# Layer B's Strassen blocks in a written order, with sums by adding DMA

## The chip, the cores and the metric

The kernel runs on one core of a Trainium2 chip. The metric is the device time of one execution in microseconds (us). TensorE (PE) multiplies, VectorE (DVE), ScalarE (ACT) and GpSimd (POOL) work elementwise, SyncE (SP) issues DMAs; ACT and GpSimd issue some, too. Everything is in float32.

## The reference

Two layers, each h = h + W_out(mixer(RMSNorm(h)) * silu(z)), and a last RMSNorm. The sequence has 1024 tokens, the model 1024 channels, the inner width is 2048. Layer A gates chunks of 128 tokens; layer B is a Mamba-2 mixer. What matters here is the input projection of layer B and what stands right behind it:

```python
proj = h @ w_in                                   # 1024 x 1024 times 1024 x 6176
z = proj[..., :D_INNER]                           # gate: silu(z)
xbc = proj[..., D_INNER:D_INNER + B_CONV_DIM]     # x, B and C
dt_raw = proj[..., D_INNER + B_CONV_DIM:]
xbc = jax.nn.silu(causal_depthwise_conv(xbc, conv_w, conv_b))   # 4 taps along the tokens
dt = jax.nn.softplus(dt_raw + dt_bias)            # then cumulative sums and decays per chunk of 128
```

Then a scan over eight chunks in eight groups uses x, B, C, dt and silu(z), a group norm follows, and the output projection.

## The kernel before, in words

A float32 product is made of three matmuls: each operand is split into a high part (a cast, `split`, L106, ACT) and a low part (source minus high part, VectorE; L112), and `mm3` (L131) adds high x high, high x low and low x high in PSUM.

The projections of layer A and most of layer B's are done in **blocks** of Strassen-Winograd (class `Block`, L182). A block multiplies four quarters of the weights, b[kh, j] (each 512 rows by 256 columns, one tile of 128 x 4 x 256 from a ring of four `wr` slots, L193), with quarters and sums of quarters of the transposed, normalized activations (A11 to A22, S1 to S4; high and low part, fourteen tiles out of the sixteen slots of tag s8). Instead of eight products there are seven, numbered 1 to 7, each of two **units** of twelve matmuls (128 x 128 x 512). Seven products need weight sums: t1 = b01 - b00 (L204, product 5), t2 = b11 - t1 (L205, product 6), b10 - t2 in place (L212, product 4), b11 - b01 in place (L214, product 7). `prep` (L207) makes the sums that a product needs, casts and subtracts; `mm` (L222) runs a unit; `post` (L247) copies a PSUM partial result to SBUF (`u`, L252, products 1, 6 and 7) or hands a finished quarter to `done` (products 2, 4, 5 and 3). Products 1, 6, 7 and 4 add up in the same two PSUM banks, 5 and 3 in two others, 2 in two of its own. `run` (L264) loads the four quarters and takes the products in the order 1, 2, 6, 7, 4, 5, 3.

Layer B has eight such blocks:

- gate blocks 0 to 3 (`z_block`, L905; `zb`), whose `done` adds the two partial results (VectorE, L913), applies silu (ACT, L915) and stores to `z_d` by a DMA that GpSimd issues (L917). Gate block 3 has half the columns (one unit per product);
- x, B and C blocks for two pairs of groups (`xbc_block`, L1214; an x block and a B/C block for each pair). Their `done` adds (VectorE, L1240), copies a halo of three columns (ACT, L1244) and puts a convolution on the list `todo`: one ACT instruction (L1211), three taps on VectorE (L1205, each with a small halo instruction L1208 for the second half of the tokens), silu on ACT (L1234) and a store that ACT issues (L1235). Two of the eight convolutions of a block read their input straight from PSUM. `convolve` (L1196) does one from the list.

`into_b` (L959), the end of layer A, gate block 0, and products 1 of gate block 1, is one `manual_schedule`: each engine takes its instructions in the order in which they are written. What follows (L1191, L1192 and L1335 to L1347) is left to the compiler's scheduler, which picks an order for each engine: the rest of gate block 1 with `decays` (L1142, small vectors from dt) behind product 6, gate block 2, then x pair 0, B/C pair 0, x pair 1, gate block 3, B/C pair 1, with a convolution before each unit from x pair 0 on. Gate block 1 and 2 make their sums on VectorE, the later ones on GpSimd, where gate block 3 also makes its low parts. `rest_a21` (L1257) reloads and splits A21. Up to LEFT = 4 convolutions are left for the scans. Then comes a new PSUM pool (L1348), the projections that are not done by Strassen (`projections`, L1274, tile `ab`) and the scans (L1570), written out by hand again.

In layer A's and B's output projection (class `Out`, L618) there are already sums by DMA: `add` (L701, L702) issues from GpSimd a DMA with `accum_op`, which adds its source to the destination, and L699 and L667 negate a tile on ACT for it.

Names: P = 128; tag k2 has three slots (tiles zt, xc), q4 six (u), wh and wl three each. `tk` holds per-token vectors for the scans in an s8 slot to the end.

## Time and profile before

| | us |
|---|---|
| median of 3 runs (1626.3 to 1628.99) | 1627.37 |
| the profiled execution | 1622.94 |
| its span, first to last instruction | 1621.2 |
| TensorE busy | 1514.6 |
| VectorE, ACT, GpSimd busy | 1085.5, 757.0, 466.8 |

Times in rows count from the start of the span. A row of a group gives line, engine, operation, output<-inputs, shapes and count, then busy us and mean ns of one, then the idle time of the engine just before them and what ended it. A row of a timeline gives start, length, engine and instruction; in brackets the idle time before it. A row of waits gives who waited for whom: us in total, times, longest. A row with three figures between strokes gives the shortest, median and longest duration in ns.

### The profile page before, as it was taken

The page shows a single profiled execution, that of the slowest core. Times are in us where ns is not written, and L with a number is a line of the kernel's source. Part 1 is how long each engine was busy: PE and PEld are TensorE (multiplying, and loading weights), DVE is VectorE, ACT ScalarE, POOL GpSimd, SP SyncE. Part 2 cuts the span into 40 slices and gives each one's busy share as a digit, 9 for nine tenths or more (in the row PEclk, how much of TensorE's full clock was granted, in tenths as well). Part 3 has the DMA queues.
Part 4 walks back from the last instruction along what each step waited for, and adds up shares of the span by engine and source line. Part 5 has one row for each costly group of instructions (what it writes and reads, how often), then busy time and mean ns, then how long its engine had stood idle before and what let it go on. Part 6 is the DMA issues. An engine that isn't in the chain of part 4 may idle for free. (4 is left out here: it accounts for less than half of the span.)

```text
span 1621.2 us, 21245 instructions
## 1 busy us (share of the span) xinstructions
PE 1514.6 (93%) x7832; PEld 1246.8 (77%) x7832; DVE 1085.5 (67%) x1669; ACT 757.0 (47%) x1239; POOL 466.8 (29%) x477
## 2 busy tenths in 40 slices
PE   5899999999999999997899998999999999889988
PEld 4799988888888878775678776777777767657776
DVE  6966566666666545577743788587777777657646
ACT  4522232333223345554543454456666576544454
POOL 3601110000000131234203223316766766221231
PEclk9899999999999999998999999999999999979999
DMA  5153333233334999932253222547666665795993
GB/s 171 44 185 135 106 98 109 101 104 109 109 109 167 297 263 238 191 104 65 83 108 113 83 98 85 175 134 206 172 173 183 171 188 143 228 239 179 223 241 113
DMA packets 164872, 244.89 MB, mean 151 GB/s; under 512 B 16048, under 2 KB 96800, under 8 KB 161568
## 3 DMA queue, kind: packets, MB, share of 16 engines
q1 hardware_dynamic: 134672, 166.43, 34.1%
q0 software_dynamic: 20928, 63.45, 17.2%
q10 hardware_dynamic: 9168, 13.64, 2.3%
q8 instruction: 62, 1.02, 0.3%
q14 instruction: 42, 0.34, 0.1%
HBM read 169.23 MB, written 51.18 MB: 136 GB/s over the span
## 5 line engine op out<-in xcount | busy, mean ns | idle before, releaser
L134 PE MATMUL acc<-hh,wh 128*128 128x512 f32 x868 | 345.3, 398 | 14.5 <-ACT wh L111 4.2
L135 PE MATMUL acc<-hl,wh 128*128 128x512 f32 x868 | 342.8, 395 | 4.4 <-DVE hl L989 4.4
L136 PE MATMUL acc<-hh,wl 128*128 128x512 f32 x868 | 342.5, 395 | 3.8 <-DVE wl L112 3.0
L112 DVE TENSOR_TENSOR wl<-wr,wh 128x1024 fp32r<-128x1024 f32 x94 | 122.9, 1310 | 128.8 <-ACT wh L111 128.8
L134 PEld LDWEIGHTS acc<-hh,wh 128*128 128x128 f32 x868 | 165.8, 191 | 52.0 <-DVE u L1240 5.2
L136 PEld LDWEIGHTS acc<-hh,wl 128*128 128x128 f32 x868 | 165.8, 191 | 41.3 <-DVE wl L112 4.8
L135 PEld LDWEIGHTS acc<-hl,wh 128*128 128x128 f32 x868 | 165.9, 191 | 38.7 <-DVE hl L989 4.8
L111 ACT CAST wh<-wr 128x1024 fp32r<-128x1024 f32 (+1 forms) x113 | 116.2, 1030 | 115.8 <-PE acc L135 78.7
L252 ACT COPY u<-acc 128x512 f32<-128x512 f32 x117 | 68.0, 582 | 187.2 <-PE acc L136 185.9
L136 PE MATMUL acc<-wh,hl 128*128 128x256 f32 x448 | 131.3, 293 | 11.5 <-DVE hl L355 11.5
L134 PE MATMUL acc<-wh,hh 128*128 128x256 f32 x448 | 132.1, 295 | 4.2 <-DVE vt L291 2.5
L135 PE MATMUL acc<-wl,hh 128*128 128x256 f32 x448 | 130.7, 292 | 1.1 <-DVE wl L365 1.1
L1424 ACT ACTIVATE wl<-wl,tk 128x128 f32<-128x128 f32 x256 | 82.1, 391 | 88.2 <-DMA wl<-cs_d 87.7
L134 PE MATMUL ab<-hh,wh 128*128 128x512 f32 x256 | 115.5, 451 | 2.2 <-DVE u L1240 2.2
L136 PE MATMUL ab<-hh,wl 128*128 128x512 f32 x256 | 100.8, 394 | 0.0
L135 PE MATMUL ab<-hl,wh 128*128 128x512 f32 x256 | 100.1, 391 | 0.0
L136 PEld LDWEIGHTS acc<-wh,hl 128*128 128x128 f32 x448 | 89.9, 201 | 12.5 <-DVE hl L355 12.5
L134 PE MATMUL bo<-wh,xh 128*128 128x512 f32 x192 | 80.9, 421 | 14.6 <-ACT wh L111 5.7
L134 PEld LDWEIGHTS acc<-wh,hh 128*128 128x128 f32 x448 | 90.0, 201 | 5.2 <-issue 2.9
L112 DVE TENSOR_TENSOR xl<-ya,xh 128x1024 fp32r<-128x1024 f32 x40 | 49.1, 1228 | 64.3 <-ACT xh L111 64.2
L135 PEld LDWEIGHTS acc<-wl,hh 128*128 128x128 f32 x448 | 90.0, 201 | 1.6 <-DVE wl L365 1.4
L605 POOL DMA_DIRECT2D y_d<-y x8 | 4.4, 548 | 291.8 <-DVE y L602 291.8
(316 smaller groups left out, 3379.6 us busy)
## 6 DMA issues: line engine op xcount, KB each, us to landing
wr<-in_a_w_in_dram SPq DMA_DIRECT2D x48, 512.0 KB, 3.6
wl<-cs_d SPq DMA_DIRECT2D x64, 256.0 KB, 3.6
wr<-in_b_w_in_dram SPq DMA_DIRECT2D x30, 512.0 KB, 4.8
ya<-ya POOLq DMA_DIRECT2D x28, 512.0 KB, 14.7
wb<-in_a_w_out_dram SPq DMA_DIRECT2D x10, 1024.0 KB
wb<-in_b_w_out_dram SPq DMA_DIRECT2D x10, 1024.0 KB, 18.2
wr<-in_b_w_in_dram SPq DMA_DIRECT2D x36, 256.0 KB, 4.4
v<-v_d SPq DMA_DIRECT2D x8, 1024.0 KB, 4.9
```

Source lines behind the costliest of these rows:

```text
L111: nc.scalar.copy(out=hi, in_=src)
L112: return (eng or nc.vector).tensor_tensor(out=lo, in0=src, in1=hi.bitcast(F32), op=ALU.subtract)
L134: nc.tensor.matmul(out=o, lhsT=l[0], rhs=r[0], start=start, stop=False, **kw)
L135: nc.tensor.matmul(out=o, lhsT=l[0], rhs=r[1], start=False, stop=False, **kw)
L136: nc.tensor.matmul(out=o, lhsT=l[1], rhs=r[0], start=False, stop=stop, **kw)
L252: nc.scalar.copy(out=self.u[n][:, i], in_=a)
L605: store = lambda: nc.gpsimd.dma_start(out=y_d[-1], in_=y)
L1424: nc.scalar.activation(wl[:, j, :], wl[:, j, :], AF.Relu, scale=-1.0, bias=tokc(2, c, self.g)[:, j:j + 1])
```

## The change

The blocks of layer B behind gate block 0 are written out by hand with into_b in one `manual_schedule`. The order of blocks becomes gate 1, x pair 0, gate 2, B/C pair 0, gate 3, x pair 1, B/C pair 1; that of the products 1, 2, 6, 7, 5, 4, 3. Each product's cast and low part are written one product ahead. The sums are made by DMA, begun in the block before: `sums_a` (at product 7) negates b01 into t2 and in place on ACT and adds b00 to t2 and b11 to b01; `sums_b` (at product 5) negates b00 into t1 and adds b01 to it, and b11 to t2; `fourth` (at the block's own product 2) writes -t2 over b10 and adds b10 again from HBM. The weights of the next block are loaded between its products. t1 and t2 share one s8 tile, t12, in all blocks; those of gate block 1 are issued at the end of into_b. Gate stores of blocks 1 to 3 are issued by ACT instead of GpSimd. A convolution is begun in every second unit, and its silu and store follow in the next unit (`late`). `decays` and `rest_a21` become generators whose pieces stand between units; the tiles of `decays` move from s8 to q4. LEFT becomes 3.

```diff
 class Block:
+        def add(self, dst, kh, j):
+            o = 0
+            for w in self.W(kh, j):
+                n = w.shape[1]
+                nc.gpsimd.dma_start(out=dst[:, :, o:o + n], in_=w.rearrange("(k p) n -> p k n", p=P),
+                                    accum_op=ALU.add)
+                o += n
+        def sums_a(self):
+            b12 = self.b[0, 1]
+            t12 = s8([P, 2, 4, 256], "t12")
+            self.t1, self.t2 = (t12[:, i, :, :self.cols] for i in range(2))
+            nc.scalar.mul(self.t2, b12, -1.0)
+            nc.scalar.mul(b12, b12, -1.0)
+            self.add(self.t2, 0, 0)
+            self.add(b12, 1, 1)
+        def sums_b(self):
+            nc.scalar.mul(self.t1, self.b[0, 0], -1.0)
+            self.add(self.t1, 0, 1)
+            self.add(self.t2, 1, 1)
+        def fourth(self):
+            b21 = self.b[1, 0]
+            nc.scalar.mul(b21, self.t2, -1.0)
+            self.add(b21, 1, 0)
...
         def prep(self, n, lo=None):
+            if self.eng is not None:
+                self.sum_up(n)
...
-            nc.gpsimd.dma_start(out=z_d[g][:, m, th * 512:(th + 1) * 512], in_=zt)
+            (nc.scalar if b else nc.gpsimd).dma_start(out=z_d[g][:, m, th * 512:(th + 1) * 512], in_=zt)
...
-    SPILT, AHEAD, LEFT = (0, 1, 3, 5), 16, 4
+    SPILT, AHEAD, LEFT = (0, 1, 3, 5), 16, 3
...
         dt_post(0, pd)
+        nxt.sums_a()
+        nxt.sums_b()
         for i in range(2):
             blk.post(3, i), nxt.post(1, i)
...
-        dtw = s8([P, 6, 256], "dtw")
+        dtw = q4([P, 4, 256], "dtw")
+        cs = q4([P, 256], "cs")
...
-    zb[1].run((2, 6, 7, 4, 5, 3), {6: decays})
-    zb[2].run()
...
     def convolve():
+        while late:
+            late.pop(0)()
         if todo:
-            todo.pop(0)()
+            late.append(todo.pop(0)())
...
-            nc.scalar.activation(dst, dst, AF.Silu)
-            nc.scalar.dma_start(out=xbc_d[g][:, th, m, :], in_=dst)
+            def rest():
+                nc.scalar.activation(dst, dst, AF.Silu)
+                nc.scalar.dma_start(out=xbc_d[g][:, th, m, :], in_=dst)
+            return rest
...
-        xbc_block("x", gs).run(unit=convolve)
-        if gs[0]:
-            zb[3].eng = nc.gpsimd
-            zb[3].run(unit=convolve, lo=nc.gpsimd)
-        xbc_block("bc", gs).run(behind={6: rest_a21, 5: lambda: next(pj)} if gs[0] else {},
-                                unit=convolve)
+    def blocks():
+        ORDER = (1, 2, 6, 7, 5, 4, 3)
...
+        bs = [zb[1], xbc_block("x", pairs[0]), zb[2], xbc_block("bc", pairs[0]), zb[3], xbc_block("x", pairs[1]),
+              xbc_block("bc", pairs[1])]
+        seq = [(k, n) for k in range(len(bs)) for n in ORDER]
+        small, turn, a21 = decays(), [0], rest_a21()
+        def between():
+            turn[0] += 1
+            if next(small, 0) == 0 and turn[0] % 2:
+                convolve()
+            else:
+                while late:
+                    late.pop(0)()
+        for at, (k, n) in enumerate(seq[1:], 1):
+            b, nxt = bs[k], bs[k + 1] if k + 1 < len(bs) else None
+            if at + 1 < len(seq):
+                k2_, n2 = seq[at + 1]
+                if n2 not in bs[k2_].Y:
+                    bs[k2_].prep(n2)
+            if n == 2:
+                b.fourth()
+            if nxt is not None:
+                if n == 1 or at == 1:
+                    nxt.load(0, 1)
+                if n == 6:
+                    nxt.load(0, 0)
+                elif n == 7:
+                    nxt.sums_a()
+                elif n == 5:
+                    nxt.load(1, 0)
+                    nxt.sums_b()
+                elif n == 4:
+                    nxt.load(1, 1)
+            elif n == 7:
+                next(a21)
+            elif n == 4:
+                next(a21, None)
+                next(pj)
+            for i in range(b.units):
+                between()
+                b.mm(n, i)
+        while len(todo) > LEFT:
+            convolve()
+    with tc.manual_schedule():
+        into_b()
+        blocks()
     next(pj)
-    while len(todo) > LEFT:
-        convolve()
```

More of the change, by code (lines that the diff above doesn't have):

```diff
@@ L207, in prep, with sum_up @@
         def prep(self, n, lo=None):
+            b = self.b
+            if self.eng is not None:
+                self.sum_up(n)
+            src = {1: b[0, 0], 2: b[1, 0], 4: b[1, 0], 7: b[0, 1], 3: b[1, 1]}.get(n)
+            if src is None:
+                src = self.t1 if n == 5 else self.t2
+            h_, l_ = wh([P, 4, self.cols]), wl([P, 4, self.cols])
+            split(h_, l_, src, lo)
+            self.Y[n] = (h_, l_)
+        def sum_up(self, n):
             b, TT = self.b, self.eng.tensor_tensor
@@ L1134 @@
     zb[0].eng, zb[0].wide = nc.gpsimd, True
-    with tc.manual_schedule():
-        into_b()
     tok_of = {}
@@ L1147, in decays @@
         nc.scalar.activation(e_, e_, AF.Exp)
+        yield
         V.tensor_scalar(s_, e_, 2.0, None, ALU.add)
@@ L1153, in decays @@
         for k in range(7, 0, -1):
+            if k == 4:
+                yield
             V.scalar_tensor_tensor(p_, p_, 1.0 / (2 * k + 1), s2, ALU.add, ALU.mult)
+        yield
         V.scalar_tensor_tensor(p_, p_, 1.0, s_, ALU.add, ALU.mult)
@@ L1187, in decays @@
             nc.scalar.copy(out=tok[:, i], in_=tp[:, 0:256].rearrange("p (c r) -> p c r", c=2))
+            yield
         nc.sync.dma_start(out=decb, in_=dec_d.rearrange("c h -> (c h)").partition_broadcast(P))
         tok_of.update(tok=tok, decb=decb)
-    zb[1].run((2, 6, 7, 4, 5, 3), {6: decays})
-    zb[2].run()
-    xbc_d, todo = {}, []
+    xbc_d, todo, late = {}, [], []
     def convolve():
+        while late:
+            late.pop(0)()
         if todo:
-            todo.pop(0)()
+            late.append(todo.pop(0)())
     def conv_ops(dst, src, ch, halo=None):
@@ L1259, in rest_a21 @@
         nc.sync.dma_start(out=raw, in_=f01_d)
+        yield
         H2.update(new_H(("A21",)))
@@ L1590, in scans @@
         project(AHEAD // 2 + 1)
-        while todo:
+        while todo or late:
             convolve()
```

22 lines of the change are left out of this document (8 added, 14 removed).

## The prediction

> **What bounds the kernel now.** I read the page first, then the windows over the stage that the diff touches, then TensorE's waits there, then the order of time around one wait.
>
> ```profile
> span 1621.2 us, 21245 instructions
> PE 1514.6 (93%) x7832; PEld 1246.8 (77%) x7832; DVE 1085.5 (67%) x1669; ACT 757.0 (47%) x1239; POOL 466.8 (29%) x477
> ```
> TensorE is busy 93% of the span, so a gain has to come out of its holes. The stage runs from the second product of gate block 1 to the first matmul of the projections:
>
> ```profile
> 799.80:1066.90 267.10, 250.93 (x1075) 203.15 (x1073) 178.84 (x234) 125.66 (x191) 68.76 (x49) 0.98 0.39 113
> ```
> ```profile
> 799.14 0.39 PE L134 MATMUL acc<-hh,wh 128*128 128x512 f32 x1
> ...
> 799.82 0.39 PE L134 MATMUL acc<-hh,wh 128*128 128x512 f32 x1
> ...
> 830.55 0.39 PE L136 MATMUL acc<-hh,wl 128*128 128x512 f32 x1
> 834.54 0.80 PE L134 MATMUL acc<-hh,wh 128*128 128x512 f32 x1 [3.60 <-DVE zt L913]
> 835.13 0.63 PE L135 MATMUL acc<-hl,wh 128*128 128x512 f32 x1
> ...
> 837.56 0.40 PE L135 MATMUL acc<-hl,wh 128*128 128x512 f32 x1
> ```
> The columns of the window are us, then busy time of PE, PEld, DVE, ACT, POOL, then clock, DMA share and GB/s. The code issues 89 units of 12 matmuls here (12 of gate block 1, five full blocks of 14, 7 of the half-size gate block 3): 1068. The two rows at 799 are three matmuls apart, 0.68/3 = 0.227 us each at full clock, so the stage needs 242.4 us. It takes 267.1: **24.7 us are lost**, and no more can be won here. The rows from 830.55 on show what a loss is made of: 7.01 us to 837.56 where eight matmuls need 1.81, that is 5.2 lost, of which 3.60 idle and 1.6 in matmuls that run at about half the clock behind the hole (0.63 in place of 0.39).
>
> ```profile
> PE acc L134 <- DVE u L1240: 4.0, 3, 2.9
> PE acc L134 <- DVE zt L913: 3.6, 1, 3.6
> PE acc L134 <- ACT wh L111: 2.8, 1, 2.8
> PE acc L134 <- ACT u L252: 2.7, 2, 1.6
> PE ab L134 <- DVE u L1240: 2.2, 1, 2.2
> ```
> These waits sum to 15.3; slow matmuls behind three of them, six transposes (1.2) and short hitches make up the rest. Their releasers are post-processing and casts, not VectorE's or GpSimd's sums as such.
>
> **The change part by part.** Durations that the steps use (busy, mean ns, idle before):
>
> ```profile
> L111 ACT CAST wh<-wr 128x1024 fp32r<-128x1024 f32 x31 | 32.3, 1049 | 29.5 <-PE acc L135 21.6 <-POOL t L204 2.4 <-PE acc L136 2.2
> L252 ACT COPY u<-acc 128x512 f32<-128x512 f32 x38 | 22.0, 579 | 16.3 <-PE acc L136 15.1 <-ACT xc L1234 1.2
> L1211 ACT ACTIVATE xc<-u,par 128x512 f32<-128x512 f32 x22 | 17.8, 811 | 2.9 <-DMA xbc_d<-xc 2.4 <-ACT xc L1234 0.4
> L1234 ACT ACTIVATE xc<-xc 128x512 f32<-128x512 f32 x28 | 17.7, 631 | 41.7 <-DVE xc L1208 34.3 <-DVE xc L1205 7.4
> L913 DVE TENSOR_TENSOR zt<-acc,u 128x512 f32<-128x512 f32 x15 | 10.2, 686 | 17.8 <-DMA z_d<-zt 10.5 <-PE acc L136 7.3
> L112 DVE TENSOR_TENSOR wl<-wr,wh x10: 1212/1221/1227, 780.2 to 850.6; 128x1024 fp32r<-128x1024 f32 x10
> L699 ACT ACTIVATE wb<-wb x8: 1061/1062/1065, 596.3 to 1505.7; 128x1024 f32<-128x1024 f32 x8
> ```
> *Sums.* Four tensor_tensor per block leave GpSimd and VectorE. In their place come four negating copies on ACT (1.06 each, the L699 row) and five adding DMAs. VectorE's other work gains by that, too:
>
> ```profile
> 907.53 2.83 POOL L214 TENSOR_TENSOR wr<-wr 128x1024 f32<-128x1024 f32 x1
> ```
> ```profile
> 908.04 2.33 DVE L1208 SCALAR_TENSOR_TENSOR xc<-halo,par,xc 128x2 f32<-128x2 f32 x1
> 910.30 0.74 DVE L1205 SCALAR_TENSOR_TENSOR xc<-u,par,xc 128x509 f32<-128x509 f32 x1
> 910.96 0.21 DVE L1208 SCALAR_TENSOR_TENSOR xc<-halo,par,xc 128x3 f32<-128x3 f32 x1
> 911.09 0.73 DVE L1205 SCALAR_TENSOR_TENSOR xc<-acc,par,xc 128x511 f32<-128x511 f32 x1
> ```
> The two-column end of a tap took 2.33, until GpSimd's sum was through; the next one 0.21. So I count a tap with its halo at 911.09-910.30 = 0.79 and without at 910.96-910.30 = 0.66: three make 2.4 and 2.0. Without the GpSimd sums VectorE has no other reason to be slow, and no price of its own in the sum.
>
> *Entry.* The new sums of block 1 start only at the end of into_b, behind dt_post on ACT:
>
> ```profile
> 793.78 1.03 ACT L953 ACTIVATE dtr<-part,hv 32x256 f32<-32x256 f32 x2 [1.28 <-DVE part L950]
> ```
> ```profile
> L702 POOL DMA_DIRECT2D wb<-wb x16: 831/1190/3217, 574.9 to 1520.5; - x16
> ```
> ```profile
> wb<-wb POOLq DMA_DIRECT2D x2, 512.0 KB, 6.7
> ```
> ```profile
> DMA to landing us min/median/max: 4.6/14.0/24.2
> ```
> The first negation ends at 794.8+1.1 = 795.9. t2 then needs two adds in a row, the second waiting on GpSimd for the first. No add runs in this stage yet: over the whole kernel the landings range from 4.6 to a median of 14.0. The DMA is busy 0.39 of this stage, so I take the 6.7 of the window from 1440 to 1480, nearer to the short end. t2 is whole at 809.3; the cast (1.05) and low part (1.22) of product 6 end at 811.6, while product 2 ends on TensorE at 799.8+24x0.227 = 805.2. That is 6.4 idle and 1.6 of slow clock, **8 us** that before does not have (2.2 with landings of 4.6, 23 with 14). [...] Queued behind the waiting cast on ACT stand the posts of product 2; nothing else waits for those.
>
> *Later sums* are begun a block ahead: from the step of product 5, where t1 and t2's last add are issued, to the cast of product 6 lie four products, 21.8 us, against two landings of 6.7 to 14; the fourth sum has three products, 16.3, against one negation and one landing. Hidden in full-size blocks; if landings were 14, some 1 us per block would show.
>
> *The written order.* Before, a scheduler filled ACT and VectorE; now each takes its instructions as written. What that does is seen in into_b, already written:
>
> ```profile
> 783.20 0.63 ACT L915 ACTIVATE zt<-zt 128x512 f32<-128x512 f32 x1 [7.40 <-issue]
> 786.21 0.63 ACT L915 ACTIVATE zt<-zt 128x512 f32<-128x512 f32 x1 [2.38 <-DVE zt L913]
> 786.75 1.04 ACT L111 CAST wh<-wr 128x1024 fp32r<-128x1024 f32 x1
> ```
> The first row is a silu that waits for its product; the cast of the next block at 786.75 stands behind it and behind a second silu, and starts when that is through. And a store issued by ACT costs it about 0.4:
>
> ```profile
> 933.72 0.33 ACTq L1235 DMA_DIRECT2D xbc_d<-xc  x1
> 934.09 0.59 ACT L252 COPY u<-acc 128x512 f32<-128x512 f32 x1 [0.40 <-ACT xc L1234]
> ```
> The gate stores move there from GpSimd. A product lasts 24x0.227 = 5.45. In gate block 2 six of the seven products also carry a convolution of the block before, begun in the first unit. ACT's pass from one cast to the next is then, for products 2 and 5: cast 1.05, negation 1.06, convolution's first 0.81, taps 2.4 and VectorE's add 0.69 (the silu behind them waits), three silus with stores 3x1.03 = **9.1**. Product 7: cast 1.05, low part 1.22 (t12 has one free slot beside fourteen activation tiles and tk, so the negation waits for the last reader), two negations 2.1, 0.81, 2.4, silu and store 1.03, copy 0.58 = 9.2. Product 4: 1.05+1.22+2.4+2x1.03 = 6.7. Products 1 and 6: 1.05+1.22+2.0+1.03+0.58 = 5.9. Product 3: 5.45. Sum 51.3 against 38.1: 13.2 late, less the 2.3 by which a low part is early at the start: 10.9. The single waits that this makes, product by product, are at most some 3.5 us, of the size of the idle above; I count one slow clock for them, 1.6, and take **12 us** (6 if the waits overlap half as much, 18 with a slow clock behind four). Gate block 3 has products of 2.72, with four convolutions and the full-size negations of the next block: casts 7x0.6 (an estimate: half of 1.05 and some start-up), negations 0.6+3x1.06, copies 3x0.58, outputs 4x1.03, convolutions 4x1.84 = 21.2 of ACT in 19.1 of TensorE, 2 us over even without a wait; with the same waits on taps and on t12, which come four times in half the time, I take **8 us** (4 to 14).
>
> [...]
>
> ```profile
> 912.48 0.80 PE L134 MATMUL acc<-hh,wh 128*128 128x512 f32 x1 [2.89 <-DVE u L1240]
> 913.08 0.63 PE L135 MATMUL acc<-hl,wh 128*128 128x512 f32 x1
> ```
> *The rest.* In the four x/B/C blocks ACT has no silus of its own: 2 us in all (0 to 6). The transposes stay at 1.2. The hand-over stays near its 2.2 to 2.6 (to 10 if three convolutions written ahead of the projections hold PSUM). The small vectors of the decays fit into the units; as many table loads as before come with them.
>
> *Sum.* 8+12+8+2+1.2+2.6 = 33.8 lost instead of 24.7: **9 us slower**. Outside the stage I take nothing: one convolution fewer is left over. The profiled execution took 1622.94 (span 1621.2), so 1632; the median of the three runs lies 4.4 above it, so 1636 in their terms.
>
> **The rivals.** (a) *ACT's queue keeps up.* It decides at passes of 5.45+2.3/7 = 5.8 on average in the gate blocks. For it: ACT was busy only 125.66 of 267.10, and one adds roughly 28 of negations and 10 of stores, 61%. Against it: the passes above are latency, not load. Then 12 and 8 shrink to 2 each, 18 lost, 7 faster; with landings of 4.6 at the entry and none in the gate blocks 2.2+2+1.2+2.6 = 8 lost, 16 faster: 1611 to 1620. (b) *The sums land late*: landings of 14 give entry 23 and 1 us in each of six blocks, 21 more: 1657. Against it: 0.39 of DMA share. (c) *Even*: the losses trade, 24.7 again, 1627. (d) *The sums are not begun a block ahead*, because a slot of the weights comes free a product later than written: three products, 16.3, then stand against two landings, 13.4, still hidden, so 1636; it is in the forecast's chance.
>
> **How the numbers follow.** Forecast 0.48; (a) 0.32; (b) 0.08; (c) 0.12. A measurement tells about 0.2% (3.3 us) from no change, so (c) is "same": faster 0.32, same 0.12, slower 0.56. The range leaves out (b) and the far end of (a): 1613 to 1650. The forecast alone: 1631 to 1650.
>
> **What would show it.** Right: TensorE waits at about 805 for a cast of t2; waits on ACT casts and low parts in gate blocks 2 and 3, none to speak of in x/B/C; ACT idle behind the taps. Wrong: gate block 2 at 39 us; GpSimd's adds landing past 10 us; slow clock in x/B/C blocks; or time moved in the scans.

## The result and the profile after

| us | before | after |
|---|---|---|
| median of 4 runs each on one chip | 1626.84 (1623.89 to 1628.99) | 1673.03 (1668.48 to 1675.64) |
| ratio | 1 | 1.0282 (95%: 1.0253 to 1.0312) |
| span of the profiled execution | 1621.2 | 1673.8 |
| from the last dt matmul (L978, before L943) to the first projection matmul | 278.2 | 327.2 |
| behind it | 554.3 | 558.4 |

The change is slower by 46 us, against 9 forecast: outside the range of 1613 to 1650. The two profiled executions lie further apart than the medians: of 52.6 us more span, 49.0 lie in the stage and 4.1 behind it (-0.5 ahead). The page of the changed kernel begins:

```profile
span 1673.8 us, 21300 instructions
PE 1521.9 (91%) x7832; PEld 1249.4 (75%) x7832; DVE 1052.5 (63%) x1668; ACT 784.3 (47%) x1267; POOL 456.4 (27%) x475
```
TensorE has the same 7832 matmuls, VectorE and GpSimd 43 us less work between them, ScalarE 27 more. Nothing is busier that could be the new bound; TensorE waits. Since the order is now fixed, I can cut the stage at block borders by counting matmuls, and read the windows (us, busy time of PE, PEld, DVE, ACT, POOL, clock, DMA share, GB/s):

```profile
799.40:836.60 37.20, 26.44 (x103) 20.31 (x102) 15.92 (x28) 19.08 (x24) 9.20 (x9) 0.86 0.86 157
836.60:860.60 24.00, 13.79 (x52) 10.40 (x51) 3.84 (x4) 4.99 (x8) 0.00 (x0) 0.79 1.02 156
860.60:898.70 38.10, 38.10 (x170) 31.55 (x169) 15.48 (x18) 17.49 (x25) 6.39 (x5) 1.00 0.65 131
898.70:949.30 50.60, 42.86 (x170) 33.25 (x168) 25.80 (x44) 26.67 (x36) 11.61 (x9) 0.93 0.75 163
949.30:988.30 39.00, 38.47 (x168) 31.55 (x169) 17.81 (x21) 16.72 (x27) 7.74 (x6) 1.00 0.54 99
988.30:1015.20 26.90, 21.90 (x86) 16.43 (x85) 14.32 (x23) 15.53 (x24) 6.38 (x5) 0.94 0.74 154
1015.20:1058.70 43.50, 40.17 (x170) 32.49 (x169) 25.32 (x39) 23.84 (x34) 11.66 (x9) 0.96 0.85 169
1058.70:1115.40 56.70, 38.21 (x169) 31.34 (x168) 40.34 (x62) 27.91 (x41) 4.93 (x3) 0.86 0.63 171
```
The rows are: products 2, 6, 7, 5 of gate block 1 (96 matmuls), its products 4 and 3 (48), x pair 0 (168), gate block 2 (168), B/C pair 0 (168), gate block 3 (84), x pair 1 (168), B/C pair 1 with the hand-over (168). At 0.227 us a matmul they lose **15.5, 13.1, 0, 12.5, 1.0, 7.8, 5.4 and 18.7 us**, 74.0 in all. The waits of TensorE in that stretch name the engines (us in total, times, longest):

```profile
PE acc L134 <- ACT wh L111: 28.7, 7, 10.2
PE ab L134 <- DVE xc L1248: 18.5, 1, 18.5
PE acc L134 <- ACT u L287: 6.7, 3, 3.1
PE acc L136 <- DVE wl L112: 2.1, 4, 0.5
```
Four places, seen in timelines of the changed kernel (start, length, instruction; in brackets the idle time before it). **The entry**, on GpSimd, ScalarE and TensorE:

```profile
795.75 1.33 POOL L201 DMA_DIRECT2D t<-in_b_w_in_dram  x1 [4.40 <-ACT t L210]
...
801.99 1.26 POOL L201 DMA_DIRECT2D t<-in_b_w_in_dram  x1 [2.31 <-DMA t<-in_b_w_in_dram]
```
```profile
811.52 1.04 ACT L111 CAST wh<-t 128x1024 fp32r<-128x1024 f32 x1 [11.37 <-DMA t<-in_b_w_in_dram]
```
```profile
812.62 0.80 PE L134 MATMUL acc<-hh,wh 128*128 128x512 f32 x1 [7.65 <-ACT wh L111]
```
t2's second add is issued 6.2 us after the first, for which it waits, and the cast starts 9.5 after that; TensorE stands 7.65 us. **The hole behind it**, on ScalarE (ACTq is its DMA issue):

```profile
834.78 0.63 ACT L950 ACTIVATE zt<-zt 128x512 f32<-128x512 f32 x1
842.06 0.34 ACTq L952 DMA_DIRECT2D z_d<-zt  x1
...
842.71 0.63 ACT L950 ACTIVATE zt<-zt 128x512 f32<-128x512 f32 x1
851.04 0.33 ACTq L952 DMA_DIRECT2D z_d<-zt  x1
851.41 1.04 ACT L111 CAST wh<-wr 128x1024 fp32r<-128x1024 f32 x1 [8.06 <-DMA dec_d<-dtw]
```
The two gate stores that moved to ScalarE are issued 6.7 and 7.7 us after their activations. The semaphores in the trace say why. The 543 DMA instructions of SyncE and ScalarE carry eight of them in turn (67 or 68 each), and each of the two stores was issued right after the transfer that had carried its semaphore before it had landed, 0.08 and 0.07 us behind. For the first store that is a 32 KB store of the decays (issued at 833.92, landed at 841.98), for the second one of 0.1 KB (840.14, landed at 850.97). The next factor's cast stands behind, and TensorE for 10.2 us. **Gate block 2** shows the passes that the prediction worked out:

```profile
920.24 0.63 ACT L1279 ACTIVATE xc<-xc 128x512 f32<-128x512 f32 x1 [2.42 <-DVE xc L1248]
...
924.09 1.06 ACT L210 ACTIVATE t<-wr 128x1024 f32<-128x1024 f32 x1 [1.29 <-DVE wl L112]
...
936.89 0.63 ACT L950 ACTIVATE zt<-zt 128x512 f32<-128x512 f32 x1 [3.13 <-DVE zt L948]
```
**The hand-over**, on ScalarE, VectorE and TensorE; L1254 begins a convolution:

```profile
1098.91 0.81 ACT L1254 ACTIVATE xc<-u,par 128x512 f32<-128x512 f32 x1 [0.40 <-ACT xc L1279]
...
1103.44 0.78 ACT L1254 ACTIVATE xc<-acc,par 128x512 f32<-128x512 f32 x1 [0.41 <-ACT xc L1279]
...
1107.69 0.81 ACT L1254 ACTIVATE xc<-u,par 128x512 f32<-128x512 f32 x1 [0.41 <-ACT xc L1279]
...
1112.13 0.78 ACT L1254 ACTIVATE xc<-acc,par 128x512 f32<-128x512 f32 x1 [0.41 <-ACT xc L1279]
```
```profile
1112.94 2.32 DVE L1248 SCALAR_TENSOR_TENSOR xc<-acc,par,xc 128x511 f32<-128x511 f32 x3 [1.94 <-ACT xc L1254]
```
```profile
1115.41 0.76 PE L134 MATMUL ab<-hh,wh 128*128 128x512 f32 x1 [18.50 <-DVE xc L1248]
```
Four convolutions, one every 4.4 us (1112.13-1098.91 = 13.2 for three), each engine waiting for the other; the last of them reads PSUM, and the projections' pool waits for that.

### The profile page after: what moved, and what is told of

The parts are those of the page before. It is cut to its first block, busy times and chain, and to the rows that moved or that the text cites. A ratio compares the mean times of both kernels' runs of the same rounds, so it can differ in the third digit from the quotient of the medians.

```text
span 1673.8 us, 21300 instructions
## 1 busy us (share of the span) xinstructions
PE 1521.9 (91%) x7832; PEld 1249.4 (75%) x7832; DVE 1052.5 (63%) x1668; ACT 784.3 (47%) x1267; POOL 456.4 (27%) x475
## 3 DMA queue, kind: packets, MB, share of 16 engines
q8 instruction: 62, 1.02, 0.2%
## 4 chain that ended last, share of the span: by engine, by line
PE 54%; DMA 16%; DVE 11%; issue 8%; ACT 8%; POOL 2%; SPq 1%; ACTq 0%; POOLq 0%; DVEq 0%
PE acc L136 12%; PE acc L134 12%; PE acc L135 12%; DMA wl<-cs_d 5%; PE ab L134 2%; PE ab L136 2%; PE ab L135 2%; DMA ya<-ya 2%; DMA wb<-wb 2%; DVE xc L1248 2%; PE mx L630 2%; PE yy L1540 2%; DVE wl L112 2%; ACT wh L111 1%; DMA dec_d<-dtw 1%
## 5 line engine op out<-in xcount | busy, mean ns | idle before, releaser
L136 PE MATMUL acc<-hh,wl 128*128 128x512 f32 x868 | 346.1, 399 | 5.2 <-DVE wl L112 5.2
L112 DVE TENSOR_TENSOR wl<-wr,wh 128x1024 fp32r<-128x1024 f32 (+1 forms) x99 | 120.9, 1222 | 167.2 <-ACT wh L111 167.2
L136 PEld LDWEIGHTS acc<-hh,wl 128*128 128x128 f32 x868 | 167.3, 193 | 45.9 <-DVE wl L112 10.5
L136 PE MATMUL acc<-wh,hl 128*128 128x256 f32 x448 | 131.0, 293 | 10.4 <-DVE hl L390 10.4
L134 PE MATMUL ab<-hh,wh 128*128 128x512 f32 x256 | 116.4, 454 | 18.5 <-DVE xc L1248 18.5
L136 PEld LDWEIGHTS acc<-wh,hl 128*128 128x128 f32 x448 | 89.8, 200 | 11.3 <-DVE hl L390 11.3
L111 ACT CAST xh<-ya 128x1024 fp32r<-128x1024 f32 x40 | 42.1, 1052 | 89.5 <-PE ao L135 39.1
## 6 DMA issues: line engine op xcount, KB each, us to landing
wb<-in_b_w_out_dram SPq DMA_DIRECT2D x10, 1024.0 KB, 19.2
```

The lines of the kernel that those rows point to most:

```text
L111: nc.scalar.copy(out=hi, in_=src)
L112: return (eng or nc.vector).tensor_tensor(out=lo, in0=src, in1=hi.bitcast(F32), op=ALU.subtract)
L134: nc.tensor.matmul(out=o, lhsT=l[0], rhs=r[0], start=start, stop=False, **kw)
L136: nc.tensor.matmul(out=o, lhsT=l[1], rhs=r[0], start=False, stop=stop, **kw)
```

## The experiments

**Theory A:** separate places where engines that follow a written order stand behind each other: late sums at the entry, stores on slots held by the small decay stores, casts behind taps in the gate blocks, convolutions ahead of the projections. **Theory B:** the adding transfers and their negations are the price everywhere. Later names: C, the gate's own last pass; D, the chain per convolution. The table gives what each place loses, worked out as above (hand-over with B/C pair 1; a wait ahead of a block's first matmul counts for that block), the stage and what lies behind. The last dt matmul starts at 784.4 to 790.9 us from build to build, so the stage is compared and not the span. The part behind scatters, too: seven versions that leave hand-over and scans as they are (vec1, zpool1, spread, declate, unit2, zlate, engsum) have 554.6 to 561.4 there, so a few us of difference in it tell nothing by themselves.

| | products 2, 6, 7, 5 | 4, 3 | x 0 | gate 2 | B/C 0 | gate 3 | x 1 | hand-over | stage | behind |
|---|---|---|---|---|---|---|---|---|---|---|
| changed kernel | 15.5 | 13.1 | 0 | 12.5 | 1.0 | 7.8 | 5.4 | 18.7 | 327.2 | 558.4 |
| handover | 15.3 | 13.5 | 0 | 12.4 | 1.2 | 7.7 | 5.4 | 6.0 | 314.8 | 564.8 |
| front3 | 15.4 | 12.6 | 0 | 12.5 | 1.1 | 8.0 | 5.6 | 6.0 | 314.5 | 567.4 |
| pipe | 15.5 | 12.6 | 0 | 12.5 | 1.5 | 7.8 | 5.3 | 15.1 | 323.5 | 555.3 |
| vec1 | 2.0 | 16.2 | 0 | 12.4 | 0.6 | 8.0 | 2.3 | 18.7 | 313.3 | 559.4 |
| zpool1 | 15.2 | 0.3 | 10.3 | 12.3 | 1.1 | 7.7 | 4.4 | 18.7 | 322.9 | 559.1 |
| spread | 14.8 | 1.1 | 15.2 | 10.9 | 4.3 | 7.6 | 5.1 | 18.6 | 330.8 | 554.6 |
| declate | 14.9 | 0 | 0.8 | 12.2 | 0.9 | 7.8 | 5.2 | 18.9 | 313.9 | 561.4 |
| unit2 | 15.5 | 13.5 | 0 | 6.0 | 1.3 | 8.5 | 3.5 | 18.7 | 320.0 | 556.0 |
| nogate | 15.2 | 13.9 | 0 | 7.4 | 2.4 | 11.1 | 7.7 | 24.2 | 335.4 | 556.3 |
| zlate | 14.7 | 2.6 | 3.7 | 7.9 | 6.4 | 4.1 | 4.5 | 18.7 | 315.8 | 560.0 |
| engsum | 2.0 | 5.8 | 1.5 | 11.3 | 1.7 | 5.8 | 3.2 | 18.7 | 303.2 | 558.1 |
| all4 | 2.0 | 0.2 | 11.4 | 7.4 | 0 | 8.1 | 2.7 | 6.0 | 291.0 | 568.4 |
| eng_best | 1.5 | 0 | 0.8 | 7.4 | 4.9 | 11.7 | 9.6 | 27.5 | 316.5 | 558.5 |
| add_best | 1.5 | 0 | 3.3 | 8.5 | 2.4 | 11.0 | 5.3 | 24.5 | 309.7 | 559.5 |
| combo_a | 3.8 | 0 | 3.4 | 1.7 | 0.3 | 3.2 | 3.4 | 6.0 | 275.1 | 563.0 |
| combo_e | 3.8 | 0 | 0.8 | 2.7 | 0 | 3.4 | 4.2 | 6.0 | 274.1 | 559.8 |
| combo_f | 3.9 | 0 | 0.8 | 2.7 | 0 | 2.9 | 4.1 | 6.8 | 274.4 | 559.4 |

### The hand-over: handover, front3, pipe

```diff
handover:
-    SPILT, AHEAD, LEFT = (0, 1, 3, 5), 16, 3
+    SPILT, AHEAD, LEFT = (0, 1, 3, 5), 16, 6
handover and front3:
-                todo.append(lambda: out(0, i, j, a))
+                front = kind == "bc" and gs[0] and u is None
+                todo.insert(0 if front else len(todo), lambda: out(0, i, j, a))
pipe, in convolve:
-        while late:
+        while len(late) > 1:
             late.pop(0)()
-        if todo:
-            late.append(todo.pop(0)())
+        rest = todo.pop(0)() if todo else None
+        while late:
+            late.pop(0)()
+        if rest:
+            late.append(rest)
```


> Leaves six convolutions instead of three for the scan stage and puts the two that still read PSUM at the front of the list. Theory A (the hand-over waits for a chain of about 4.4 us per convolution, of which the last that reads PSUM ends the 18.5 us wait of the first projection matmul): the wait falls to 3 to 8 us, the stage from gate block 1's product 2 to the first projection matmul gets 10 to 15 us shorter, and the time falls from 1673 to 1659-1664, less what the three convolutions cost in the scans (0 to 4 us). Rival (the exchange of the PSUM pools or the projections' own weights hold that matmul): the wait stays within 3 us of 18.5 and the time within 3 us of 1673. The other losses (entry 15, product 5 to 3 of gate block 1 13, gate blocks 2 and 3 13 each) stay by both.

> Only the order of the list: the two convolutions that read PSUM stand at its front, and three are left as in the changed kernel. Theory A (the first projection matmul waits because those two hold PSUM; the others can run beside the projections): its wait of 18.5 us falls to 5 to 9 us as with six left, the part behind (558.4 us) stays within 3 us, so stage and part together lose 8 to 13 us. Rival (the price is the number of convolutions that are run one after the other ahead of the projections' own evictions): the wait falls, but the part behind grows by as much, and the sum of both stays within 4 us.

> A convolution's first pass is issued ahead of the last pass of the one before it instead of behind it; nothing else. Theory D (the list is a serial chain, ScalarE, VectorE, ScalarE, of 4.4 us for each, though VectorE is busy for 2.3 to 2.9 of it): the four convolutions of the hand-over take 2.4 to 3.0 us each, the wait of 18.7 us falls to 10 to 14, and the part behind (558.4 us) falls by 0 to 6 us, both kept; the time falls by 6 to 13 us. Rival (each waits for its store's slot, or ScalarE and VectorE share the limit): the wait stays above 16.

handover took 12.4 us out of the stage, as theory A had it, but gave 6.4 back behind it, more than the 0 to 4 expected. front3, with the number of convolutions unchanged, gained 12.7 and gave 9.0 back: the sum fell by 3.7, and that is the rival. Its waits show where the time reappears:

```profile
PE yy L1541 <- DVE wl L1533: 8.8, 1, 8.8
PE ab L134 <- ACT xc L1279: 5.9, 1, 5.9
```
The convolutions still run one after the other beside the projections, and the first scan matmul (yy) waits 8.8 us instead (9.0 in handover; no such wait in the changed kernel). So holding PSUM mostly chose the place where the chain is paid. pipe aims at the chain itself: the wait fell to 14.9 us, short of the 10 to 14 expected, and nothing came back behind (555.3). What limits it then is on ScalarE:

```profile
PE ab L134 <- DVE xc L1251: 14.9, 1, 14.9
```
```profile
1104.03 0.81 ACT L1257 ACTIVATE xc<-u,par 128x512 f32<-128x512 f32 x1 [3.12 <-DMA xbc_d<-xc]
```
The next convolution waits for a store to leave one of the three k2 slots. Theory D holds in part: the order within the chain is worth 3.6 us of the wait, and the rest of the 18.5 stays, with another reason. (front3 gave 9.0 back and handover 6.4; that difference is within the scatter.)

### The entry: vec1

```diff
-        nxt.sums_a()
-        nxt.sums_b()
...
+    zb[1].eng, zb[1].wide = nc.vector, True
...
-            if n == 2:
+            if n == 2 and b.eng is None:
                 b.fourth()
```


> The sums of gate block 1, the first one that is run by the written order, are formed by VectorE instead of by adding DMA; all other blocks stay as in the changed kernel. Theory A (the entry loses 15 us because the first adding transfers are issued at 795.8 us and the sum is whole only at 811.5, with TensorE idle from 804.6 to 812.6, and ScalarE runs late behind them): the loss from 799 to 836 us falls to 0 to 4 us and the time to 1659-1663. Rival (VectorE, which also has the decays and the outputs of the block before, is the next bound there, or the fall of the clock has another cause): the loss stays above 8 us.

The entry's 15.5 became 2.0, theory A. The stage fell by 13.9; the hole behind came earlier and grew to 16.2.

### The hole: zpool1, spread, declate

```diff
zpool1:
-            (nc.scalar if b else nc.gpsimd).dma_start(out=z_d[g][:, m, th * 512:(th + 1) * 512], in_=zt)
+            (nc.scalar if b > 1 else nc.gpsimd).dma_start(out=z_d[g][:, m, th * 512:(th + 1) * 512], in_=zt)
spread, at the end of the loop over q that issues the small stores:
-        yield
+            yield
+            yield
declate, ahead of that loop:
+        for _ in range(10):
+            yield
```


> The stores of gate block 1's outputs go back to GpSimd's queue; those of gate blocks 2 and 3 stay on ScalarE's. Theory A (ScalarE stood 10.17 us with two stores that wait for slots of the hardware queues which SyncE's small decay stores hold, each 8 to 11 us in flight, and the split of the next factor stood behind them): the loss of 13.1 us between 836 and 870 us falls to 0 to 3 us and the time to 1659-1664. Rival 1 (ScalarE is short of work time there, stores or not): the loss stays above 8 us. Rival 2 (the stores now wait on GpSimd behind the four adding transfers, or hold these up): the loss moves to the x block behind it, and the time stays within 4 us of 1673.

> The sixteen small stores of the decays are issued in four groups of four, two units of work apart, instead of all in one; the gate's stores stay on ScalarE's queue. Theory A (ScalarE's store waits for one of the eight slots of the hardware queues that the small stores hold for 8 to 11 us each): the hole of 10.33 us at 842 falls to 0 to 3 us, the stage from 327.2 to 313-319 us. Rival (the DMA engines themselves are full there, share 0.80 of them between 836 and 870 us against 0.44 before, so that stores are late in any order): the hole stays above 6 us, at this place or a product later.

> The decays' sixteen small stores are issued ten units of work later, in the x block, and with them the transposes; the adding transfers and the gate's stores on ScalarE's queue stay. Spreading them changed nothing (the hole came 5.7 us later, 10.56 us long), and without adding transfers it was 3.02 and 1.37 us with the small stores in place. Theory A (small stores and adding transfers together: the one is slow in flight, the other fills the engines): without the small stores the hole of 10.33 us falls to 0 to 4 us. Theory B (the adding transfers alone hold the gate's stores): the hole stays at 7 to 12 us. Either way the small stores may show up in the x block, where 0 us is lost now.

zpool1 shows that the engine that issues the gate's stores is not the main cause: 0.3 us is left in products 4 and 3, but 10.3 come up ahead of the x block's first product (rival 2 in the place, if not in the reason it gave). GpSimd issues the stores without a wait for the small ones, but three of them, from 833 to 838 us, land only after 15.8 to 17.5 us, and ScalarE waits for one of the three k2 slots:

```profile
ACT zt L950 <- DMA z_d<-zt: 12.8, 1, 12.8
```
spread missed in the same way: the hole came 5.7 us later, also ahead of the x block, and grew (three gate stores 16.5 to 21.1 us in flight, ScalarE's wait for a k2 slot 14.4). declate took it away, but for 0.8 in the x block. With the adds in place, this window of declate has TensorE busy without a break at a DMA share of 0.79 (the changed kernel has 1.02 from 836 to 862 us), and the gate stores from 815 to 870 us land in 2.0 to 7.4 us; the row has the one landing that it could tell:

```profile
836.00:862.00 26.00, 26.00 (x117) 21.52 (x116) 9.33 (x10) 11.19 (x16) 2.92 (x3) 1.00 0.79 173
```
```profile
z_d<-zt ACTq DMA_DIRECT2D x8, 256.0 KB, 6.1
```
So adding transfers at that share don't make the hole by themselves; the small stores among them do. Without adds and their negations, but with the small stores in place, it is shorter: 5.8 in engsum (below) against 16.2 in vec1, with the same early entry. In the kernel before, the same eight small stores took as long, and the three gate stores issued beside them (821 to 828 us) 7.1 to 12.1 us, and no cast stood behind a store on ScalarE's queue. But VectorE's addition waited for a k2 slot that the first of the three held (landed at 833.67), and that is the hole of 5.2 us at 834.54 from which the prediction worked out what a loss is made of:

```profile
dec_d<-dtw SPq DMA_DIRECT2D x8, 0.1 KB, 9.5
```
```profile
833.79 0.69 DVE L913 TENSOR_TENSOR zt<-acc,u 128x512 f32<-128x512 f32 x1 [7.56 <-DMA z_d<-zt]
```

### The gate blocks: unit2, nogate, zlate

```diff
unit2:
-            if next(small, 0) == 0 and turn[0] % 2:
+            if next(small, 0) == 0 and second:
...
-                between()
+                between(i == 1 or b.units == 1 and turn[0] % 2 == 0)
nogate:
-            if next(small, 0) == 0 and turn[0] % 2:
+            if next(small, 0) == 0 and b not in zb:
zlate, in z_block's done:
-            nc.scalar.activation(zt, a, AF.Silu)
-            (nc.scalar if b else nc.gpsimd).dma_start(...)
+            def rest():
+                nc.scalar.activation(zt, a, AF.Silu)
+                (nc.scalar if b else nc.gpsimd).dma_start(...)
+            late.append(rest) if b else rest()
```


> In blocks of two units per product the convolution is begun in the second unit of every product instead of in each second unit counted over all, that is, its taps have the time of the next product's first unit; gate block 3, of one unit per product, is left as it was. Theory A (gate block 2 loses 13.5 us because ScalarE's in-order passes stand behind taps that were begun just before: 3.13, 2.42 and 1.29 us): gate block 2's loss falls to 2 to 7 us, gate block 3's stays at 10 to 15, and the time falls to 1660-1668. Rival 1 (adding transfers or weights that land late hold TensorE in the gate blocks): gate block 2's loss stays at 11 to 16 and the time at 1670-1676. Rival 2 (the passes only change places): the loss moves into the x and B/C blocks, which lose nothing now.

> Convolutions are begun in each unit of the x and B/C blocks and in none of the gate blocks; all else as in the changed kernel. Theory A (taps and passes of convolutions are what ScalarE's casts stand behind in gate blocks 2 and 3, 13.5 and 13.2 us, and too few convolutions are done by the end of the last block, so that four stand ahead of the projections): gate blocks 2 and 3 lose 3 to 7 us each, the x and B/C blocks 0 to 4 in all, the hand-over 3 to 9 instead of 18.7; the stage from the last dt matmul to the first projection matmul falls from 327.2 to 295-308 us and the part behind it stays at 555 to 560. Rival (the adding transfers, with 35 to 66% of the DMA engines, hold the gate blocks): these stay at 10 to 14 each and the stage above 310. Second rival (a convolution per unit is too much for ScalarE beside the casts): the x and B/C blocks lose over 8 us.

> The gate's last pass (ScalarE's activation and its store) is put off by one unit of work, as the convolutions' last pass is, so that ScalarE no longer stands behind VectorE's addition of the two halves. Theory C (gate blocks 2 and 3 lose 12.5 and 13.2 us, the latter with the first product behind it, because ScalarE waits 8.2 us in three waits in each for that addition with the next factor's cast behind it): gate block 2 falls to 2 to 7 us, gate block 3 with the product behind it to 5 to 9, the stage from 327.2 to 311-320 us. Rival 1 (convolutions begun in the first unit are the cause): the falls are under 3 us each. Rival 2 (the accumulators are now held a unit longer, and TensorE waits for these): new waits of TensorE for the activation, and the stage is not shorter than 325.

unit2 halved gate block 2 (6.0) and helped x pair 1. nogate fell: gate block 2 still lost 7.4, gate block 3 even more (11.1), and with a convolution in each unit the blocks behind and the hand-over lost up to 5.5 us more. With no convolution begun in it, ScalarE still stands in gate block 2 behind VectorE's addition of the two halves:

```profile
ACT zt L950 <- DVE zt L948: 9.6, 5, 2.5
```
(TensorE's own waits there are another matter: 4.0 us for VectorE's low parts, 0.9 for casts.) zlate puts that pass off. It reached the expected stage by another way than I had said: the hole fell to 6.3 (2.6 and 3.7 in the x block) as the stores come a unit later, gate block 3 with x pair 1 fell from 13.2 to 8.6, but gate block 2 only moved: 7.9, with 6.4 now ahead of and in B/C pair 0 (12.5 and 1.0 in the changed kernel). Theory C fails for gate block 2 taken alone: one pass put off, the taps still hold the next (ScalarE waits 17.2 us for them). The versions that have both edits, combo_a and combo_e, bring it to 1.7 and 2.7; they have four others as well, and the pair was not run alone.

### The sums: engsum, eng_best, add_best

```diff
engsum, in blocks and into_b (adds and fourth left out):
+            if n == 1:
+                b.sums()
...
-        return Block(H2, W, False, done, None, wide)
+        blk = Block(H2, W, False, done, nc.vector if b < 3 else nc.gpsimd, wide)
...
-        return Block(H2, W, False, done, None)
+        b = Block(H2, W, False, done, nc.gpsimd)
```
eng_best is engsum, nogate and declate in one kernel, add_best vec1, nogate and declate.

> The written order with the blocks in turn stays, but all sums are formed by an engine (VectorE for gate blocks 1 and 2, GpSimd for the others) a product ahead, from factors that are loaded as before; no adding DMA and none of ScalarE's five negations of a block. Theory A (the losses are the order's: convolutions before projections, ScalarE's stores behind the small stores, passes behind taps): only the entry falls, 15 to 0-4 us, the hole at 842 stays at 8 to 14 us, gate blocks 2 and 3 at 9 to 14 each, the hand-over at 18.7; the stage is 309 to 316 us. Theory B (the adding transfers are the cost: q0 holds 35 to 66% of the DMA engines in these parts, and the negations take 5.3 us of ScalarE in each block): gate blocks 2 and 3 fall below 6 each and the hole below 5; the stage is 278 to 300 us.

> Three edits together on the changed kernel: sums by an engine, no adding DMA; convolutions in each unit of the x and B/C blocks alone; the decays' small stores ten units later. Theory B (the adding transfers are a cost of their own, some 9 us at the hole and 15 at the entry, and bring nothing that the written order wouldn't): this is the fastest version, with a stage of 268 to 282 us (303.2 with the sums alone changed, less 14 of the hand-over, 6 to 14 of the gate blocks and 0 to 4 of the hole), a part behind of 554 to 560 and a ratio to the kernel before of 0.985 to 1.000. Theory A (the sums by DMA are no cost once begun early enough): it is no faster than the version with adding transfers, within 4 us.

> The same with the adding transfers kept for all blocks but gate block 1, whose sums VectorE forms: convolutions in each unit of the x and B/C blocks alone, the decays' small stores ten units later. Theory A (adding transfers cost nothing once begun a block ahead; order and convolutions did the harm): stage 268 to 282 us, ratio 0.985 to 1.000, as without them. Theory B (they fill the DMA engines and take five negations of ScalarE in each block): 5 to 15 us longer than the version with sums by an engine, in the gate blocks and at the hole; ratio 0.997 to 1.008.

engsum lies between the theories: the entry and half of the hole are gone (stage 303.2), gate block 2 and the hand-over stay. (A block has four negations, L210, L211, L216 and L223, 4.2 us of ScalarE, not the five and 5.3 us of the expectations.) Both combinations missed their ratios (1.0262 and 1.0231, 95%: 1.0240 to 1.0283 and 1.0205 to 1.0256), and nogate is in both: the hand-over loses as much as there or more (27.5 and 24.5, nogate 24.2). Against each other they speak for theory A: with the entry and the small stores mended, the adding transfers are no dearer than sums by an engine (stage 309.7 against 316.5).

### Together: all4, combo_a, combo_e, combo_f

all4 is handover, zpool1, vec1 and unit2. combo_a is vec1, unit2, front3, declate, pipe and zlate; combo_e the same with engsum in place of vec1; combo_f is combo_e with

```diff
-                between(i == 1 or b.units == 1 and turn[0] % 2 == 0)
+                between(i == 1 or (k == 6 and n == 3) or b.units == 1 and turn[0] % 2 == 0)
```


> All four single edits together: six convolutions left with those that read PSUM first, gate block 1's stores on GpSimd, gate block 1's sums on VectorE, convolutions begun in the second unit. Alone they took 12.4, 4.3, 13.9 and 7.2 us out of the stage from the last dt matmul to the first projection matmul (327.2 us in the changed kernel, 278.2 before), and the first gave 6.4 us back in the part behind it (558.4 us). Theory A (separate places): the gains add up, the stage is 287 to 293 us, the part behind it 563 to 566, the ratio to the kernel before 1.007 to 1.013. Rival (one cause under them, the DMA engines filled by the adding transfers: what is taken away at one place comes back at the next): the stage stays above 298 us and the ratio above 1.015.

> Six edits on the changed kernel, adding transfers kept for all blocks but gate block 1: gate block 1's sums on VectorE, convolutions begun in the second unit, the PSUM readers first, the decays' small stores ten units later, convolutions overlapped, the gate's last pass a unit later. If the losses are separate places: stage 327.2 less 13.9, 13.3, 7.2, 12.5 and some 8 of the gate and the overlap, 268 to 280 us, the part behind 556 to 566, the ratio to the kernel before 0.990 to 1.005. If taking one away brings another up: ratio above 1.008.

> The same with all sums formed by an engine, no adding transfer at all. Theory A (the adding transfers cost nothing once the entry and the small stores are out of their way): within 4 us of the version that keeps them, or up to 8 us slower as between the last two of this kind (1668.2 and 1661.2 us). Theory B (they cost DMA time and five negations of ScalarE per block): 4 to 12 us faster.

> As the version with all sums by an engine and five further edits (0.9984 of the kernel before), and a convolution is begun in both units of the very last product, so that the second of the two that read PSUM is through before the last unit's own addition. Theory (program order on VectorE: the last addition stood at 1063.75 us behind 2.32 us of taps, though its matmuls had ended by 1058.7): the hand-over's wait falls from 5.9 to 1 to 4 us, some slow clock goes with it, and the ratio is 0.994 to 0.998. Rival (the exchange of the PSUM pools has a floor): the wait stays at 5 to 6.5 us and the ratio at 0.997 to 1.000.

all4's stage is the sum of the single gains (291.0; 289.4 by adding up), but its ratio, 1.0147 (1.0113 to 1.0180), missed theory A's by what came back behind (568.4). And the hole lies ahead of x pair 0, as in zpool1: the gate's stores, on GpSimd's queue once more, held a slot:

```profile
ACT zt L950 <- DMA z_d<-zt: 15.2, 1, 15.2
```
combo_a and combo_e come out level with the kernel before: 0.9988 (0.9967 to 1.0009) and 0.9984 (0.9968 to 0.9999). So the added loss is undone place by place with order and sums by DMA kept (combo_a, but for gate block 1's sums), and whether the sums are made by DMA or by an engine makes no difference that can be told. TensorE's waits in combo_e's stage:

```profile
PE ab L134 <- ACT xc L1289: 5.9, 1, 5.9
PE acc L136 <- DVE wl L112: 5.7, 5, 2.7
PE acc L134 <- ACT u L287: 3.2, 3, 1.9
PE acc L134 <- ACT xc L1289: 0.5, 1, 0.5
```
combo_f went for the 5.9 and missed: 1.0002 (0.9989 to 1.0015), and the wait is 6.7. VectorE's row in combo_e, then in combo_f:

```profile
1063.75 0.68 DVE L1297 TENSOR_TENSOR u<-acc,u 128x512 f32<-128x512 f32 x1
```
```profile
1062.29 2.31 DVE L1258 SCALAR_TENSOR_TENSOR xc<-u,par,xc 128x511 f32<-128x511 f32 x3
1064.51 0.69 DVE L1297 TENSOR_TENSOR u<-acc,u 128x512 f32<-128x512 f32 x1
```
The last addition came no earlier (by the stage's own start 0.3 us later): the second unit began one more convolution, whose taps stand ahead of it. So it was no test of a floor in the pool exchange; that stays open, as does a version that is clearly faster than both.

## Why the prediction was wrong

Its direction came out, its size did not: 33.8 us lost by its sum, 74.0 measured. Two steps failed most, the hand-over and the decays' small stores, which it put at nothing; a third, the entry, was too small. Term by term:

| term | predicted | measured |
|---|---|---|
| entry | 8 | 15.5 |
| products 4 and 3 of gate block 1 | 0 | 13.1 |
| gate block 2 | 12 | 12.5 |
| gate block 3, with its posts in x pair 1 | 8 | 13.2 |
| x, B and C blocks | 2 | 1.0 |
| transposes | 1.2 | in the first two rows |
| hand-over | 2.6 | 18.7 |

- **The hand-over** is the term that was furthest off, 18.7 against 2.6: "near its 2.2 to 2.6 (to 10 if three convolutions written ahead of the projections hold PSUM)". The condition in brackets came true, with four convolutions, and each costs a latency of 4.4 us where I had counted 1.84 of ScalarE's time and 2.0 to 2.4 of VectorE's. The working for gate block 2 had the pattern already: silu waits for taps, the next first pass waits for silu. And the chain has to be paid somewhere: with the PSUM readers ahead (front3) 9.0 us of it came back behind.
- **The decays' small stores** were put at nothing: "The small vectors of the decays fit into the units". Their instructions do. But most of their sixteen stores are 8 to 11 us in flight, gate stores beside them are late as well, and that is the 13.1 in products 4 and 3 that no term and no rival held. The kernel before already lost 5.2 in this way, and the prediction's row of L913 named the store ("<-DMA z_d<-zt 10.5"), but it read the hole as VectorE's post-processing. Ten units later (declate) it is 0, with 0.8 in the x block. The gate stores' move to ScalarE, priced at 0.4 us of issue, only decided what waits: there the next issue, for a semaphore; with the stores on GpSimd (zpool1) the next silu, for a slot. Undoing it moved the hole and took 2.5 us off.
- **The entry** was right in mechanism (TensorE waits from 804.97 for a cast of t2, which is whole at 811.5 instead of 809.3) and under-sized: second landing 9.5 instead of 6.7, a second wait of 3.1 us on ScalarE, and more slow clock (0.86 over the stretch). The four issues were 1.3 to 1.9 us, where the adds of the kernel before had 0.8 to 3.2 (L702), so long issues are not what was late.
- **Gate block 2** was hit, 12.5 against 12, with the right waits of ScalarE worked out beforehand, but in part by luck: TensorE stood 7.8 us there (4.0 for casts, 2.7 for a copy, 1.1 for low parts) where 10.9 were counted, and two spells of half clock, 3.41 us each, cost some 3.4 us where one of 1.6 was counted; the two errors nearly cancel. unit2 shows that the taps are half of it; that the gate's own passes are the rest is argued from ScalarE's waits and from the versions that have zlate, too. **Gate block 3** lay inside its bounds of 4 to 14 with the 5.4 of x pair 1, whose one long wait of TensorE (2.80, for the cast at 1022.51) stands behind gate block 3's last silu (1021.48).
- **"Even" and "ACT's queue keeps up"** fell; so did "the sums land late" as the general price: the adds landed 4.6 to 19.2 us after their issue, median 6.9, beside the 6.7 that was taken, and the entry's 11.4 us on ScalarE is the only wait of a cast, copy or sum for one in the changed kernel. engsum, add_best and combo_a say the same: behind the entry the sums were on time. x, B and C blocks lost next to nothing, as said.
- "Outside the stage I take nothing" was 4.1 us off: 2.0 are there by the first scan matmul (25.4 us after the first projection matmul, before 23.4), behind slow clock (0.91 in that stretch, before 1.00). The other 2.1 are less than the scatter of that part and stay open.

## What to carry to other kernels

When a piece of work that a scheduler placed is written out by hand, price each piece by its latency through all engines (4.4 us for a convolution that keeps none busy for 3), and look for what stands behind it in each queue. A store can wait before it is issued (6.7 and 7.7 us here) and hold its slot after it (12.8 in zpool1): before tiny stores are put among large transfers, look at how long both are in flight and who needs the next slot. On an engine with casts in its queue, what stands behind such a store waits along (here a cast, and TensorE for 10.2 us). And a wait removed at one end of a chain that nobody shortened can come back at the other end (9.0 of 12.7 us in front3), so count the span and not the hole.

## What the runs showed of the hardware

The clock fell after shorter idle times than the 3.60 and 2.89 us that I had rows for. In gate block 2 of the changed kernel 1.52 us of idle, and 0.53 two matmuls on, left it whole; after 2.45 us, and 0.52 two matmuls on, it fell, 1.6 us behind the longer wait:

```profile
932.15 0.50 PE L134 MATMUL acc<-hh,wh 128*128 128x512 f32 x1 [1.52 <-ACT wh L111]
...
933.75 0.39 PE L134 MATMUL acc<-hh,wh 128*128 128x512 f32 x1
```
```profile
941.14 0.50 PE L134 MATMUL acc<-hh,wh 128*128 128x512 f32 x1 [2.45 <-ACT wh L111]
...
942.40 0.53 PE L136 MATMUL acc<-hh,wl 128*128 128x512 f32 x1 [0.52 <-DVE wl L112]
942.74 0.62 PE L134 MATMUL acc<-hh,wh 128*128 128x512 f32 x1
```
It stood at half from 942.73 to 946.14 us, 3.41 us, in which a matmul took 0.62 to 0.63 us where it takes 0.39 at the full clock: some 1.7 us of work. The fall behind the 2.71 us of idle ahead of 917.87 came 1.0 us after that wait, at 918.84, and also lasted 3.41 us. The longest one, 20.48 us from 1099.74 on, covers 15.7 us of the 18.50 that TensorE waits at the hand-over and the first 4.8 us of the matmuls behind it, some 2.4 us of work. These are single cases of one kernel: from what idle time on the clock falls, and for how long, they don't show.

A DMA share of 0.79 did no harm by itself (declate: no wait of TensorE there). Gate stores of 256 KB were 2.0 to 6.6 us in flight beside adding transfers alone (declate), 7.1 to 12.1 beside the eight stores of 0.1 KB and eight of 32 KB without adds (the kernel before), and 10.4 to 21.1 beside both (the changed kernel, zpool1, spread). Why such small stores are so slow, and slow others down, no run shows.
